# A hybrid S5, attention and mixture-of-experts block: a 22nd weight block, gather from x2, scatter summed in PSUM, shorter head, router and end

## The chip, the cores and the metric

One program on 1 core of a Trainium2 chip. The metric is the device time of one execution in microseconds (us). The kernel before was run three times: median 677.47 us, 676.79 to 678.37. About 0.2% (1.4 us) is what a measurement of this kernel can tell from no change. The engines are TensorE (PE, its weight loads PEld), VectorE (DVE, `V` in the code), ScalarE (ACT, `A`), GpSimd (POOL, `G`) and SyncE (SP, `DS`), which issues nearly all DMAs.

## The reference, cut to what matters

One block on 256 tokens of width 1024, all in fp32:

```python
h = rms_norm(x, ln1_g);  proj = h @ w_in                 # 1024 x 4096
# u -> S5 state-space mixer -> gelu -> glu;  q, k, v -> causal attention with a bias by distance, 8 heads
merged = sigmoid(gate_ssm) * (y_ssm @ w_up_ssm) + sigmoid(gate_attn) * (y_attn @ w_up_attn)
x = x + merged @ w_out
x = x + hier_moe(rms_norm(x, ln2_g), ...)
return rms_norm(x, ln_f_g)

def hier_moe(xf, ...):       # 4 groups x 8 experts, the best group, its 2 best experts
    for e in range(32):
        y = y + combine[:, e:e+1] * ((silu(xf @ w1[e]) * (xf @ w3[e])) @ w2[e])
```

The weights of the 32 experts (w1, w3: 1024 x 512, w2: 512 x 1024) are 192 MB, all of which are read whatever the router chooses.

## The kernel before

The kernel is one straight program; the order of each engine's instructions is that of the code. On-chip memory is cut into 23 blocks of 128 x 2048 fp32 (`blk`, tags r0 to r22), 1 MB each. A block has one user after another; a new user waits until the last reader of the old one is through. Most blocks serve the front stage first and the expert weights afterwards.

Front stage. `load_unit` (L734) loads one raw weight unit (1 MB of w_in, w_glu, w_up or w_out) into blocks 2 and 3 in turn, always two units ahead; its DMA on SP waits until the unit two before has been used. The first nine units of w_in are multiplied as fp32. The later sixteen units are split by ACT, DVE and POOL into a high and a low fp32r part (`split`, L699 and L702; `wtiles`, L748, takes blocks 4 and 6 or 5 and 7 in turn) and multiplied in three passes. Between the matmuls of a unit, `bg()` lets threads run for the S5 mixer, for the attention and for POOL. A table `KN` says which engine copies what and after how many steps a thread goes on.

Head. TensorE runs 24 warm-up matmuls on ones (L828). Then x times the gain goes to h32, half by ACT, half by DVE (L1523, L1525; ahead of it DVE runs the 13 instructions of `vexp`), and the first unit's sixteen matmuls follow, in four pairs of k (L1528).

Expert weights. `pump` (L765) takes the next 1 MB piece of the list: for each of eight quads (four experts each) sixteen w13 pieces (`k`, `t` for w1 or w3) and eight w2 pieces. It goes into the next of the 21 blocks in `KN['slots']`, in a ring. In the front stage `KN['pump']` says ahead of which half unit a piece is issued. As SP issues in order, a piece whose block isn't free holds back the raw loads behind it. In the expert stage every used piece pumps one more.

Router (from L1693). After the last quarter of the out matmuls, x2 is updated by DVE (L1700), squared by ACT for the norm (L1701), transposed by TensorE (`x2_tp`, L1708) and copied by ACT into x2T in block 5 (L1709); the logits follow (L1717). `rsqrt` (L704) is ten DVE instructions: a first guess from the bits and three Newton steps. Then the normalised h2 is written by ACT to block 7 (L1741), and the choice of group and experts is a chain of small DVE instructions (L1744 to L1775). Three matmuls (L1778 to L1780) count positions; `pos` is their product with the mask (L1782).

Expert stage (`moe_quads`, L1863). `pick` (L1829) compares positions with 1 to 32 and gives a 0/1 matrix; `gather` (L1837) multiplies h2 by it to give xg, the tokens of four experts, transposed; L1839 multiplies by the gain. `up13` (L1856) has four matmuls for each piece, into two banks pa and pb. Silu and product on ACT and DVE, four transposes, then w2 (L1903), and the scatter (L1918): the result goes back through DwT to tokens, and DVE adds it to x2 (L1919), four times a quad. Two PSUM tags of four banks are there: "a" (pa, pb, and others in the front stage) and "b" (all that passes through). In the last quad `final_part` squares x2 and multiplies it by the final gain on POOL (L1936), `final_end` (L1940 to L1949) has rsqrt, four products with it and four stores on SP. Loops for experts with over 32 tokens stand behind (L1957); in these runs they are not entered.

The functions of the change and what calls them:

Of the kernel before, what the change touches and what calls it, by code (L numbers as in the profile page):

```python
# [653 lines left out]
def hybrid_block(ctx, tc, x_ch, x_tok, small, consts, bc, w_in, w_glu, w_up, w_out, rel, onehot, w_rt, w13, w2,  # L654
# [79 lines left out]
    def load_unit(key, src, shape, parts=1):  # L734
        t = carve(blk(2 + n_raw[0] % 2, "raw"), shape[1:])[0]
# [5 lines left out]
        return t  # L741
# [4 lines left out]
    n_w = [0]  # L746
# [34 lines left out]
    sm = per.tile([128, SM_W], F32, name="sm")  # L781
# [12 lines left out]
    A.dma_start(sm, small)  # L794
# [443 lines left out]
    def norm1():  # L1238
# [5 lines left out]
        rsqrt(rtk, v1, t1, g1)  # L1244
# [274 lines left out]
    vexp(dt_, lst, pick_engine("vexp", "G", "GV"))  # L1519
    for pr in range(4):  # L1520
# [59 lines left out]
    for i, (kind, u) in enumerate(units):  # L1580
# [5 lines left out]
        if kind == "glu":  # L1586
# [9 lines left out]
            G.tensor_copy(trib, tri_f)  # L1596
# [134 lines left out]
    logits(0, range(4))  # L1731
# [314 lines left out]
```

## Time and profile before

| | |
|---|---|
| median of 3 runs | 677.47 us |
| profiled execution, its own time | 677.7 us |
| its span | 675.9 us, 9611 instructions |
| PE busy | 524.9 us (78%) |
| DVE, ACT, POOL busy | 219.9, 124.8, 135.1 us |
| DMA | 235.02 MB, mean 348 GB/s |
| weight pieces wslot | 191 of 1024 KB and 2 of 512 KB, median 19.8 us to landing |
| mean granted clock of TensorE | 0.869 |

The span is what the profiler saw of the program, the time what the device took. Busy shares are means over stages with different limits: the stage up to about 200 us is dense work on all engines, the rest is the stream of expert weights.

### The profile page before, as it was taken

How to read it: one execution, taken by the hardware profiler on the slowest of the kernel's cores; microseconds unless marked ns; L12 is line 12 of the kernel's file. 1: busy time of each engine (PE TensorE's matmuls, PEld its weight loads, DVE VectorE, ACT ScalarE, POOL GpSimd, SP SyncE). 2: the span in 40 equal slices, each digit the busy share in tenths (PEclk: the TensorE clock that was granted, in tenths of full speed). 3: DMA queues.
4: the chain of work that ended last, by engine and by line, in shares of the span. 5: the costliest groups of instructions: out<-in, count | busy, mean ns of one | idle time of the engine just before them, and what ended most of it. 6: DMA issues, size and time to landing. Idle time of an engine off the chain costs nothing. (4 is left out here: it accounts for less than half of the span.)

```text
span 675.9 us, 9611 instructions
## 1 busy us (share of the span) xinstructions
PE 524.9 (78%) x3931; PEld 292.3 (43%) x3931; DVE 219.9 (33%) x432; ACT 124.8 (18%) x281; POOL 135.1 (20%) x232
## 2 busy tenths in 40 slices
PE   9989999969998889696686757768766766676680
PEld 8878899859986443150041014104201400230130
DVE  5755889867785312120021011001101100120012
ACT  3362644464315010000000000001000000100021
POOL 4889455744561000000000000000000000000020
PEclk9989999998999899987689689766977976897685
DMA  7527343665899999999999999999999999999971
GB/s 264 199 87 248 125 157 126 250 250 193 324 369 423 406 422 420 421 420 422 420 421 421 421 422 421 420 422 420 422 421 421 420 420 422 420 422 421 420 317 68
DMA packets 35154, 235.02 MB, mean 348 GB/s; under 512 B 4051, under 2 KB 5244, under 8 KB 7452
## 3 DMA queue, kind: packets, MB, share of 16 engines
q1 hardware_dynamic: 34700, 232.51, 84.6%
q0 software_dynamic: 256, 1.74, 0.7%
q8 instruction: 33, 0.54, 0.3%
q14 instruction: 21, 0.17, 0.1%
q10 hardware_dynamic: 144, 0.06, 0.0%
HBM read 233.23 MB, written 2.63 MB: 349 GB/s over the span
## 5 line engine op out<-in xcount | busy, mean ns | idle before, releaser
L1856 PE MATMUL pb<-wslot,xg 128*32 128x512 f32 x512 | 87.1, 761 | 41.8 <-DMA wslot<-in_w 41.7
L1856 PE MATMUL pa<-wslot,xg 128*32 128x512 f32 x512 | 89.2, 777 | 38.2 <-DMA wslot<-in_w 38.2
L1936 POOL TENSOR_TENSOR ob<-x,xg 128x256 f32<-128x256 f32 (+1 forms) x6 | 5.3, 913 | 438.6 <-DMA wslot<-in_w 434.2
L1903 PE MATMUL py<-wslot,mt 128*32 128x256 f32 x1024 | 71.7, 421 | 24.5 <-DMA wslot<-in_w 18.9
L1889 DVE SCALAR_TENSOR_TENSOR mt<-mt,pa 128x512 f32<-128x512 f32 x8 | 5.5, 688 | 224.9 <-ACT mt L1888 224.9
L1856 PEld LDWEIGHTS pb<-wslot,xg 128*32 128x32 f32 x512 | 12.9, 120 | 114.8 <-DMA wslot<-in_w 104.9
L1903 PEld LDWEIGHTS py<-wslot,mt 128*32 128x32 f32 x1024 | 31.4, 119 | 64.6 <-DMA wslot<-in_w 31.6
L1856 PEld LDWEIGHTS pa<-wslot,xg 128*32 128x32 f32 x512 | 12.1, 120 | 100.4 <-DMA wslot<-in_w 88.1
L702 POOL TENSOR_TENSOR wl<-raw,wh 128x512 fp32r<-128x512 f32 (+1 forms) x22 | 40.3, 1836 | 33.8 <-ACT wh L699 18.5
L1919 DVE TENSOR_TENSOR x<-x,scp 128x512 f32<-128x512 f32 (+1 forms) x34 | 22.3, 657 | 58.7 <-PE scp L1918 58.7
L1839 DVE TENSOR_TENSOR xg<-xgp,sm 128x512 f32<-128x512 f32 (+1 forms) x18 | 11.4, 632 | 90.1 <-PE xgp L1837 90.1
L1918 PE MATMUL scp<-mt 128*128 128x512 f32 (+1 forms) x68 | 32.9, 609 | 7.1 <-ACT mt L1915 7.1
L1888 ACT ACTIVATE mt<-pa 128x512 f32<-128x512 f32 x8 | 4.8, 597 | 176.5 <-PE pa L1856 176.5
L1837 PEld LDWEIGHTS xgp<-mt,h 128*128 128x128 f32 x256 | 33.6, 214 | 6.3 <-issue 5.5
L1837 PE MATMUL xgp<-mt,h 128*128 128x128 f32 x256 | 35.5, 302 | 0.9 <-DVE mt L1829 0.9
L1915 ACT COPY mt<-py 128x512 f32<-128x512 f32 (+1 forms) x17 | 9.5, 561 | 125.8 <-PE py L1903 125.8
L702 DVE TENSOR_TENSOR wl<-raw,wh 128x512 fp32r<-128x512 f32 (+1 forms) x26 | 29.5, 1145 | 6.7 <-ACT wh L699 5.9
L1276 PE MATMUL inp<-hn,raw 128*128 128x256 f32 x128 | 29.8, 390 | 0.0
L1280 PE MATMUL inp<-hH,wh 128*128 128x256 f32 x112 | 28.2, 288 | 0.0
L1280 PE MATMUL inp<-hL,wh 128*128 128x256 f32 x112 | 27.6, 283 | 0.0
L1276 PEld LDWEIGHTS inp<-hn,raw 128*128 128x128 f32 x128 | 24.8, 197 | 4.0 <-DVE vu L1295 0.6
L699 ACT CAST wh<-raw 128x512 fp32r<-128x512 f32 (+1 forms) x28 | 20.7, 769 | 18.2 <-DMA raw<-in_w_out 7.9
(318 smaller groups left out, 745.6 us busy)
## 6 DMA issues: line engine op xcount, KB each, us to landing
wslot<-in_w SPq DMA_DIRECT2D x191, 1024.0 KB, 19.8
raw<-in_w_in SPq DMA_DIRECT2D x14, 1024.0 KB, 4.9
raw<-in_w_up SPq DMA_DIRECT2D x4, 1024.0 KB, 5.0
raw<-in_w_out SPq DMA_DIRECT2D x4, 1024.0 KB, 4.8
rbz<-rbd POOLq DMA_DIRECT2D x1, 1536.0 KB, 8.7
xc<-in_x_ch SPq DMA_DIRECT2D x4, 256.0 KB, 4.8
raw<-in_w_in SPq DMA_DIRECT2D x4, 256.0 KB, 5.8
raw<-in_w_in SPq DMA_DIRECT2D x2, 512.0 KB, 7.2
```

What stands on the lines that cost most here:

```text
L699: (A.copy if e is A else e.tensor_copy)(out_, in_)
L702: pick_engine(name, default, opts).tensor_tensor(out=out, in0=in0, in1=in1, op=op)
L1276: T.matmul(ps[:, 0:S], raws["in", u][:, k, c], (h32 if u < 3 else hn)[:, k], start=(k == 0), stop=(k == KD - 1))
L1280: T.matmul(ps[:, 0:S], (wh if x else wl)[:, k, c], (hH if y else hL)[:, k], start=first, stop=last)
L1837: T.matmul(ps[:, i * 128:i * 128 + 128], h2[:, b, k * 128:k * 128 + 128], Dt[:, b].rearrange("p e s -> p (e s)"), start=(b == 0), stop=(b ...
L1839: V.tensor_tensor(out=xg[:, ks[0]:ks[0] + n], in0=ps[:, 0:n * 128].rearrange("p (k n) -> p k n", k=n), in1=smc("g2", ks[0], ks[0] + n).uns ...
L1856: T.matmul(pab[t][32 * e:32 * e + 32], xg[:, k, 32 * e:32 * e + 32], w[:, e], start=(k == 0), stop=(k == KD - 1))
L1889: V.scalar_tensor_tensor(out=hid, in0=hid, scalar=1.0, in1=pab[0], op0=OP.add, op1=OP.mult)
L1903: T.matmul(py[32 * e:32 * e + 32, n % 2 * 256:n % 2 * 256 + 256], hidT[:, f, 32 * e:32 * e + 32], w[:, i, e], start=(f == 0), stop=(f == 3))
L1915: A.copy(ye[:, o % 512:o % 512 + m], py[:, o % 512:o % 512 + m])
L1918: T.matmul(ps[:, 0:m], DwT[:, b], ye[:, o % 512:o % 512 + m], start=True, stop=True)
L1919: V.tensor_tensor(out=x2[:, b, o:o + m], in0=x2[:, b, o:o + m], in1=ps[:, 0:m], op=OP.add)
```

## The change

- `rsqrt` is four instructions, the first a power of -0.5 on POOL (exponent in a new tile `mhalf`); the old one stays as `rsqrt_newton` for the first norm. An early small ACT instruction writes half of `mhalf`.
- 10 warm-ups instead of 24; `vexp` is emitted behind the first pair of k.
- `KN['pump']` is empty. `KN['after']` issues pieces right behind raw loads: 1 behind in9, 2 behind in11, 2 behind glu, 1 behind in15, 2 each behind up1 and up3, 1 behind out0, 2 behind out1, 1 behind out2; the rest up to the number of blocks follow the last out matmuls. The split blocks start with 5 and 7 instead of 4 and 6 (`nw`), and the ring has 22 blocks in a new order, block 7 among them.
- h2 is x2 itself; the norm's factor goes into the pick matrix (`Dts`). The counting matrix carries 512 on its diagonal, so that positions of chosen tokens lie above 512: the first pick reads them from PSUM, without the product with the mask. The index isn't cast to fp32.
- The first quad gathers k by k, and its first expert matmuls start after two of them.
- The scatter of quads 0 to 6 is summed in four PSUM banks; `sum_start`, in the last quad, adds them to x2 in a block of its own. The final gain is loaded in the last quad.
- The four stores go out in turn on SP and ACT, each behind its product.

```diff
+KN['pump'] = {}
+KN['nw'] = 1
+KN['warm'] = 10
+KN['SL'] = 1
+KN['after'] = {'in9': 1, 'in11': 2, 'glu': 2, 'in15': 1, 'up1': 2, 'up3': 2, 'out0': 1, 'out1': 2, 'out2': 1}
+KN['slots'] = [20, 16, 18, 17, 21, 19, 10, 11, 8, 22, 13, 15, 12, 14, 9, 3, 7, 2, 4, 0, 1, 6]
...
     def rsqrt(y, v, tmp, g):
+        G.tensor_tensor(out=y, in0=v, in1=mhalf, op=OP.pow)
+        V.scalar_tensor_tensor(out=g, in0=v, scalar=-0.5, in1=y, op0=OP.mult, op1=OP.mult)
+        V.tensor_tensor(out=tmp, in0=g, in1=y, op=OP.mult)
+        V.scalar_tensor_tensor(out=y, in0=tmp, scalar=1.5, in1=y, op0=OP.add, op1=OP.mult)
...
     def load_unit(key, src, shape, parts=1):
+        load_raw(key, src, shape, parts)
+        pump(KN["after"].get(key if isinstance(key, str) else "%s%d" % key, 0))
...
-    n_w = [0]
+    n_w = [KN["nw"]]
...
+    mhalf = sm[:, SM_W:SM_W + 2]
+    G.memset(mhalf, -0.5)
     warm = bank("warm", "a")
-    for i in range(24):
-        T.matmul(warm[:, 0:128], ones, ones, start=(i == 0), stop=(i == 23))
+    for i in range(KN["warm"]):
+        T.matmul(warm[:, 0:128], ones, ones, start=(i == 0), stop=(i == KN["warm"] - 1))
+    A.activation(out=mhalf[:, 1:2], in_=ones[:, 0:1], func=AF.Copy, scale=-0.5)
...
-    vexp(dt_, lst, pick_engine("vexp", "G", "GV"))
     for pr in range(4):
...
+        if pr == 0:
+            vexp(dt_, lst, pick_engine("vexp", "G", "GV"))
...
-            G.tensor_copy(trib, tri_f)
+            V.scalar_tensor_tensor(out=trib, in0=ident, scalar=511.0, in1=tri_f, op0=OP.mult, op1=OP.add)
+            G.tensor_scalar(out=iota512, in0=iota1, scalar1=511.0, scalar2=None, op0=OP.add)
...
-    logits(0, range(4))
+    logits(0, range(8))
     x2_tp(3, A.copy)
...
     rsqrt(rs2, v2, rw1, rw2)
-    logits(0, range(4, 8))
     logits(1, range(8))
...
-    V.tensor_copy(ixf, i8[:, :, 0:2])
...
-                    in1=ixf.unsqueeze(3).to_broadcast([128, 2, 2, 32]), op=OP.is_equal)
+                    in1=i8[:, :, 0:2].unsqueeze(3).to_broadcast([128, 2, 2, 32]), op=OP.is_equal)
...
-    V.tensor_tensor(out=pos.rearrange("p b e -> p (b e)"), in0=pp[:, 0:64], in1=msk.rearrange("p b e -> p (b e)"),
-                    op=OP.mult)
...
+    if SL:
+        xacc = [bank("xacc") for i in range(4)]
+        default_tag[0] = "a"
...
+        V.tensor_tensor(out=Dt, in0=iota512.unsqueeze(1).unsqueeze(1).to_broadcast([128, 2, 4, 32]),
+                        in1=(pos if at is None else at)[:, :, es].unsqueeze(3).to_broadcast([128, 2, 4, 32]),
+                        op=OP.is_equal)
+        if SL:
+            V.tensor_tensor(out=Dts, in0=Dt, in1=rs2.unsqueeze(2).unsqueeze(3).to_broadcast([128, 2, 4, 32]), op=OP.mult)
...
-                pick(qd)
-                gather(qd, (0, 1))
+                pick(qd, None if extra else pp[:, 0:64].rearrange("p (b e) -> p b e", b=2))
+                gather(qd, (0,))
+                gather(qd, (1,))
+                if not extra:
+                    V.tensor_copy(pos.rearrange("p b e -> p (b e)"), pp[:, 0:64])
+                up13(qd, pab, (0,))
                 gather(qd, (2, 3))
-                up13(qd, pab, (0,))
+                up13(qd, pab, (1,))
                 gather(qd, (4, 5))
-                up13(qd, pab, (1,))
                 gather(qd, (6, 7))
...
+                if last and SL:
+                    lnf_load()
+                    sum_start()
+                up13(qd, pab, range(2, 6))
+                if last and SL:
+                    lnf_rows()
+                up13(qd, pab, range(6, KD))
...
+                    if SL and not extra and not last:
+                        T.matmul(xacc[2 * b + o // 512], DwT[:, b], ye, start=(qd == qds[0]), stop=(qd == qds[-2]))
+                        continue
...
+    def sum_start():
+        fin["x"] = carve(blk(FIN[2], "xs"), (2, DM))[0]
+        for i in range(4):
+            b, n = divmod(i, 2)
+            c = slice(n * 512, n * 512 + 512)
+            V.tensor_tensor(out=fin["x"][:, b, c], in0=x2[:, b, c], in1=xacc[i], op=OP.add)
+        default_tag[0] = "b"
...
-        for b, o in ((0, 0), (0, 512), (1, 512), (1, 0)):
-            DS.dma_start(out[b * 128:(b + 1) * 128, o:o + 512], ob[:, b, o:o + 512])
+            (A if i % 2 else DS).dma_start(dst, x)
```

## Rows read from the trace of the kernel before

**Rows 1.** The page, part 2: DMA share in tenths, 40 slices.
```profile
DMA  7527343665899999999999999999999999999971
```

**Rows 2.** Waits of the SP queue: total us, times, longest.
```profile
SPq L774 <- DMA wslot<-in_w: 333.0, 158, 3.1
```

**Rows 3.** Stretches: busy us by engine, granted clock, DMA share, GB/s.
```profile
120.00:140.00 20.00, 17.52 (x233) 15.32 (x222) 15.38 (x21) 11.34 (x37) 15.36 (x16) 1.00 0.56 211
140.00:160.00 20.00, 16.15 (x102) 14.04 (x102) 14.26 (x27) 11.18 (x26) 5.95 (x11) 0.83 0.62 232
160.00:180.00 20.00, 20.00 (x169) 20.00 (x168) 15.36 (x22) 7.61 (x16) 10.63 (x9) 1.00 0.86 352
180.00:200.00 20.00, 19.69 (x120) 17.26 (x120) 17.63 (x24) 4.23 (x9) 13.40 (x12) 1.00 0.83 318
200.00:220.00 20.00, 16.61 (x97) 14.13 (x96) 12.07 (x40) 8.45 (x17) 3.83 (x4) 0.96 1.00 415
...
260.00:280.00 20.00, 17.30 (x138) 5.04 (x138) 3.42 (x6) 1.35 (x4) 0.00 (x0) 1.00 1.01 420
```

**Rows 4.** The tile wslot: from a piece's issue to its landing.
```profile
DMA to landing us min/median/max: 5.4/19.8/21.1
```

**Rows 5.** Timeline of SP's issues: start us, us, queue, line, xcount.
```profile
119.10 0.43 SPq L774 DMA_DIRECT2D wslot<-in_w  x1
...
191.34 0.80 SPq L774 DMA_DIRECT2D wslot<-in_w  x2
...
198.56 0.33 SPq L739 DMA_DIRECT2D raw<-in_w_out  x1
...
199.88 13.38 SPq L774 DMA_DIRECT2D wslot<-in_w  x8
...
226.39 13.82 SPq L774 DMA_DIRECT2D wslot<-in_w  x11
```

**Rows 6.** Timeline of the router, ahead of the first expert matmul.
```profile
211.61 0.59 ACT L1709 COPY x2T<-x2tp 128x512 f32<-128x512 f32 x1 [2.83 <-PE acc L1679]
...
213.63 2.99 PE L1717 MATMUL lgp<-mt,x2T 128*128 128x36 f32 x24
...
217.36 0.42 DVE L1744 SCALAR_TENSOR_TENSOR mt<-lgp,mt,sm 128x36 f32<-128x36 f32 x2
...
221.07 0.42 DVE L1829 TENSOR_TENSOR mt<-co,mt 128x256 f32<-128x256 f32 x1
...
221.65 3.69 PE L1837 MATMUL xgp<-mt,h 128*128 128x128 f32 x16 [0.87 <-DVE mt L1829]
...
225.27 1.06 PE L1856 MATMUL pa<-wslot,xg 128*32 128x512 f32 x8
```

**Rows 7.** Timeline of the head, and DVE at the attention's bias.
```profile
1.06 8.30 PE L828 MATMUL warm<-fs 128*128 128x128 f32 x48 [1.06 <-DVE fs L825]
...
4.46 1.28 ACT L1523 ACT_TABLE_LOAD   x1 [4.46 <-DMA xc<-in_x_ch]
...
7.31 0.61 DVE L1525 TENSOR_SCALAR h<-xc,sm 128x256 f32<-128x256 f32 x2
...
9.19 7.07 PE L1528 MATMUL inp<-h,raw 128*128 128x256 f32 x32
...
66.23 1.29 DVE L1347 SCALAR_TENSOR_TENSOR attA<-sc,attA 128x512 f32<-128x512 f32 x2 [1.25 <-DMA attA<-rbz]
```

**Rows 8.** Timeline of the end: last norm, products, stores.
```profile
661.42 0.33 DVE L1940 SCALAR_TENSOR_TENSOR mt<-mt 128x2 f32<-128x2 f32 x1 [0.74 <-ACT mt L1931]
...
663.90 1.28 DVE L1947 TENSOR_SCALAR ob<-ob,mt 128x512 f32<-128x512 f32 x3 [0.30 <-DVE mt L710]
...
664.41 3.59 SPq L1949 DMA_DIRECT2D out_dram<-ob  x4
```

**Rows 9.** POOL by form: busy us, mean ns of one, idle before.
```profile
L702 POOL TENSOR_TENSOR wl<-raw,wh 128x1024 fp32r<-128x1024 f32 x7 | 18.0, 2575 | 14.3 <-PE inp L1276 5.8 <-ACT wh L699 5.7 <-DVE wh L699 2.7
...
L899 POOL TENSOR_TENSOR fs<-fs 128x16 f32<-128x16 f32 x5 | 1.2, 239 | 0.4
```

More of the change, by code (lines that the diff above doesn't have):

```diff
@@ L648 @@
 }
+KN['pump'] = {}
[3 more added lines that the diff above has]
+KN['SL'] = 1
+KN['after'] = {'in9': 1, 'in11': 2, 'glu': 2, 'in15': 1, 'up1': 2, 'up3': 2, 'out0': 1, 'out1': 2, 'out2': 1}
+KN['slots'] = [20, 16, 18, 17, 21, 19, 10, 11, 8, 22, 13, 15, 12, 14, 9, 3, 7, 2, 4, 0, 1, 6]
 OPTS = {}
@@ L778, in pump @@
             ready[p] = t
-    sm = per.tile([128, SM_W], F32, name="sm")
+    sm = per.tile([128, SM_W + 34], F32, name="sm")
     co = per.tile([128, CO_W], F32, name="co")
@@ L793, in hybrid_block @@
     native = set(("in", u) for u in KN["nat"]) | set(KN["nat2"])
-    A.dma_start(sm, small)
+    A.dma_start(sm[:, 0:SM_W], small)
     for k in range(0, KD, 2):
@@ L1243, in norm1 @@
         V.tensor_scalar(out=v1, in0=ss1, scalar1=1.0 / DM, scalar2=EPS, op0=OP.mult, op1=OP.add)
-        rsqrt(rtk, v1, t1, g1)
+        rsqrt_newton(rtk, v1, t1, g1)
         for b in range(2):
@@ L1735, in hybrid_block @@
     rsqrt(rs2, v2, rw1, rw2)
-    logits(0, range(4, 8))
     logits(1, range(8))
     dump("x2", x2)
-    h2 = carve(blk(7, "h2"), (2, DM))[0]
-    for b in range(2):
-        A.activation(out=h2[:, b], in_=x2[:, b], func=AF.Copy, scale=rs2[:, b:b + 1])
+    SL, fin = KN["SL"], {"x": x2}
+    Dts = hid[:, 0:256].rearrange("p (b e s) -> p b e s", b=2, e=4) if SL else Dt
+    if SL:
+        h2 = x2
+    else:
+        h2 = carve(blk(7, "h2"), (2, DM))[0]
+        for b in range(2):
+            A.activation(out=h2[:, b], in_=x2[:, b], func=AF.Copy, scale=rs2[:, b:b + 1])
     lg = pt("lg", [128, 2, 36])
@@ L1815, in rounds, with lnf_load @@
         V.tensor_copy(nri, nrf)
-    xg, lnf = carve(blk(5, "xg"), (KD, 128), (DM,))
-    G.dma_start(lnf[0:1], ln_f)
+    if SL:
+        xacc = [bank("xacc") for i in range(4)]
+        default_tag[0] = "a"
+        xg, = carve(blk(5, "xg"), (KD, 128))
+    else:
+        xg, lnf = carve(blk(5, "xg"), (KD, 128), (DM,))
+        G.dma_start(lnf[0:1], ln_f)
+        fin["lnf"] = lnf
+    def lnf_load():
+        fin["lnf"] = carve(blk(FIN[1], "lnf"), (DM,))[0]
+        G.dma_start(fin["lnf"][0:1], ln_f)
     def lnf_rows():
+        lnf = fin["lnf"]
         for n in range(2):
@@ L1881, in moe_quads @@
                     rounds()
-                    lnf_rows()
+                    if not SL:
+                        lnf_rows()
                 up13(qd, pab, (4, 5, 6, 7))
@@ L1886, in moe_quads @@
                 back(qd)
-                up13(qd, pab, range(2, KD))
+                if last and SL:
[3 more added lines that the diff above has]
+                if last and SL:
+                    lnf_rows()
+                up13(qd, pab, range(6, KD))
             A.activation(out=hid, in_=pab[0], func=AF.Tanh, scale=0.5)
@@ L1935, in final_part @@
         for b in range(2):
-            G.tensor_tensor(out=ob[:, b, o:o + m], in0=x2[:, b, o:o + m], in1=lnf[:, o:o + m], op=OP.mult)
+            G.tensor_tensor(out=ob[:, b, o:o + m], in0=x[:, b, o:o + m], in1=lnf[:, o:o + m], op=OP.mult)
     def final_end():
@@ L1941, in final_end @@
         rsqrt(rs3, v3, rw1, rw2)
-        for b, o in ((0, 0), (1, 512), (0, 512), (1, 0)):
-            x = ob[:, b, o:o + 512]
-            if (b, o) == (1, 512):
+        for i, (b, o) in enumerate(((0, 0), (1, 512), (0, 512), (1, 0))):
+            x, dst = ob[:, b, o:o + 512], out[b * 128:(b + 1) * 128, o:o + 512]
+            if i == 1:
                 A.activation(out=x, in_=x, func=AF.Copy, scale=rs3[:, b:b + 1])
@@ L1947, in final_end @@
                 V.tensor_scalar(out=x, in0=x, scalar1=rs3[:, b:b + 1], scalar2=None, op0=OP.mult)
-        for b, o in ((0, 0), (0, 512), (1, 512), (1, 0)):
-            DS.dma_start(out[b * 128:(b + 1) * 128, o:o + 512], ob[:, b, o:o + 512])
-    FIN = [SLOTS[(n_pieces - NSLOT) % NSLOT]]
+            (A if i % 2 else DS).dma_start(dst, x)
+    FIN = [SLOTS[(n_pieces - NSLOT + i) % NSLOT] for i in range(3 if SL else 1)]
     moe_quads(range(NQ_RUN))
```

26 lines of the change are left out of this document (13 added, 13 removed).

## The prediction, made before the changed kernel was run

> **What bounds the kernel now.** I read the page's DMA line first: from the 12th of 40 slices on the DMA engines stand at 9 until the last two slices [rows 1]. Then the SP queue's own waits: 333.0 us, 158 times, are L774 waiting for an earlier weight piece [rows 2]. Then stretches: in 260 to 280 the DMA share is 1.01 at 420 GB/s [rows 3], so a 1 MB piece (1.049 MB) takes 2.50 us, and the 192 pieces of the experts take 480 of the 675.9 us. A piece lands 5.4 us after its issue at best and 19.8 in the median [rows 4]: 5.4 is 2.5 of transfer behind 2.9 of start and completion, and 19.8 is eight pieces in flight. In the expert stage only bytes count; an engine that gets faster there gives nothing. Two things can move the end: DMA time left idle before that stage, and what follows the last landing.
>
> Idle before: the DMA shares 0.56, 0.62, 0.86 and 0.83 between 120 and 200 us [rows 3] leave 20 x (0.44 + 0.38 + 0.14 + 0.17) = 22.6 us unused. By 191.7 SP has issued 11 pieces, the last raw load goes out at 198.56, and ten more pieces by 213.26. Then SP stands still until 226.39: all 21 blocks are full [rows 5]. It goes on when the first w13 piece has been used, 225.27 + 1.06 = 226.33 [rows 6]; call this moment R. Piece 22 therefore lands at 226.39 + 5.4 = 231.8. The eleven transfers issued from 198.56 on last about 198.6 + 2.4 + 11 x 2.5 = 228.5, so the rings are all but dry when R comes; share 1.00 in 200 to 220 [rows 3] says they were full until then. From R on, the time is R + 5.4 + (pieces left - 1) x 2.5 + tail, as long as a changed kernel also runs dry at R.
>
> **The change, part by part.**
>
> Head. The warm-ups are 24 matmuls in 8.30 us, and the first real matmul starts where they end, at 9.19 [rows 7]. That is 0.35 each in the mean, the early ones more; ten at 0.43 end at 5.4. What is late then: ScalarE's first scaling waits for a table load of 1.28 us until 5.76; the new small activation draws that load ahead of the data. DVE's first scaling starts at 7.31 behind the 13 instructions of vexp; it now goes ahead of vexp [rows 7]. Then vexp (13 short steps, about 2.7 us) holds the second DVE scaling until about 8.0. So the first pair of k runs from 5.4 to 7.8, the second starts at about 8.0, and three pairs of 1.77 us (7.07 / 4) end at 13.3 instead of 9.19 + 7.07 = 16.26. That is 2.9 us. If the clock is granted later than here, the first pair runs at half rate and 1.6 is left. TensorE has hardly a gap from there to 216, and most raw loads are released by it or by the splits that feed it, so the shift should travel; but the bias load of the attention hangs on POOL, which does not shift: DVE already waits 1.25 us for it at 66.23 [rows 7]. I take 2.4 of 2.9; bounds 0 and 2.9.
>
> Pieces behind raw loads. 14 pieces instead of 11 are issued before the last raw load, into the 22.6 idle us. The three extra (7.5 us) only count as far as blocks allow: with 22 blocks SP stops after piece 22, and the rings then run dry about 224.4 on the old clock (198.6 + 2.4 + 9 x 2.5 = 223.5 for the raw load and 8 pieces, and about 0.9 of gaps, because the last blocks come free only while the out matmuls end). R plus 2.9 is later, so the block count binds and the gain is one piece, 2.5 us, plus whatever R gains. Raw loads behind two pieces may land up to 2.5 us later; the places are early (in13) and late (out2), and their splits start a microsecond or more after landing, so I cost it at nothing; the price without that cover is a rival.
>
> Router. Before, the ScalarE copies of x2T wait 2.83 us for the last out matmul [rows 6], because block 5 is still a split weight; with the split blocks swapped they don't. But the transposes of the last quarter now come behind sixteen logit passes: 213.63 + 2.99 ended at 216.62 [rows 6], and I get about 216.8 after. Behind the long rsqrt lg ran from 217.36 to 217.78; with the short one its factor is ready at about 215.5, so lg ends when the logits do, at 217.2: 0.6 gained. The index cast (0.2) and the product for pos (0.26) leave the path, the product with rs2 (0.42, as the comparison at 221.07) enters it: net 0. Then the gather: 16 passes in 3.69 us, 0.23 each at half clock, all before the first expert matmul at 225.27 [rows 6]. Now only two k, eight passes, stand ahead of it: 1.8 saved. If the clock is still at half when the first four expert matmuls run, they take about 1.9 instead of 1.06: 0.9 lost. R moves by 0.6 + 1.8 - 0.9 = 1.5; bounds 1 and 3.3 (full clock in the gather).
>
> Scatter in PSUM, pick, lnf, sum_start. Four DVE additions of 0.7 us a quad go, one product of 0.42 comes, and only two banks circulate beside pa and pb; all lies under a DMA stream that keeps eight pieces ahead: 0. lnf is loaded 20 pieces, 50 us, before the end: 0.
>
> Tail. From v3 (661.42 + 0.33) to the factors (663.90 less the 0.30 of idle) ten DVE instructions take 1.85 us [rows 8]. The new chain has three of 0.2 and one on POOL. The trace has no power on POOL; a small two-input operation there takes 0.24 us, its longest 2.58 [rows 9]. A 128x2 operand is nearest to the small one; with two handovers I take 0.4, so 1.0 us instead of 1.85: 0.8 saved (bounds 0.8 and -1.5). The four stores leave SP one behind the other, 664.41 to 668.00 [rows 8], though DVE's last product ends at 663.90 + 1.28 = 665.18; an issue that waits for nothing is 0.33 to 0.43 [rows 5], four of them 1.5, so one stood about 2.1 us. With two queues the last issue ends 0.4 behind the last product, 665.6 in today's times, if nothing stands: 2.4 saved; if SP's second store stands again, about 0.7. I take 1.2. The Trainium skill (DMA: Bandwidth & Descriptors, "Issuing engines are not separate DMA queues") says that issuing from several engines saves only the sequencers' issue time, usually small beside the transfer; by it this term would be near 0 and the sum 670.2, but the 3.59 us of rows 8 are issue time, and not small.
>
> Sum, against the profiled execution (677.7, span 675.9, 1.8 around it): 2.4 + 2.5 + 1.5 + 0.8 + 1.2 = 8.4, so 669.3. The median of the three runs lies 0.2 lower: 669.0 (677.47 - 8.4 = 669.07).
>
> **Rivals.**
> *The head's shift is absorbed* by POOL's chain and the bias load: against it, TensorE itself is nearly gapless; for it, DVE's wait at 66.23. 669.0 + 2.4 = 671.4.
> *More than that*: full clock in the gather (R by 3.3 instead of 1.5) and no standing store (+1.2): 666.0. For it, the shorter idle of TensorE before the gather.
> *Late raw loads*: two places on TensorE's path pay a piece each, 5.0: 674.0. Against it, splits don't start at landing; for it, two of the raw loads come out while two pieces stand ahead of them in the rings.
> *Slower: the power on POOL.* It stands on the path twice. In the router it is free up to 1.8 us (by my estimate startable at 214.5, its result wanted at 216.9 after three short DVE steps), at the end from 0.4 on. At POOL's longest row, 2.58, the time is 669.0 + 0.8 + 2.2 = 672.0; from P - 1.8 + P - 0.4 = 8.4, so P = 5.3, the kernel is slower than before; at 6.3 it takes 679.4. No POOL row is near that. The Trainium skill (GPSIMD Engine Reference, "Instruction dispatch") puts the first call of a freshly loaded kernel at about 6 us; by that, paid once in the router, an estimate from that page is 673.2, and no run here shows such a load.
> *It doesn't do what it says*: the 22nd block fills no sooner, because a piece waits for a block and holds a raw load behind it in SP's order. Gains of head and tail are eaten: about 676.5.
>
> **Chances.** Forecast 0.53 (its own range 667 to 671), head absorbed 0.15, more 0.13, late raw loads 0.09, slow power 0.06 (slower in 0.04 of it), not as said 0.04 (half of it no change or slower). Range 665.0 to 674.0: it leaves out some of "more" and the last two. About 0.2% is what a measurement here can tell, 1.4 us. Faster 0.92, same 0.03, slower 0.05.
>
> **What would show it.** The first L1528 matmul near 5.4 and the first L1276 near 13.3; SP with 14 pieces ahead of the last raw load and 8 behind it; the first L1856 matmul about 3.9 earlier (2.4 + 1.5) than 225.27, and a dip of DMA share below 1 just after it; the last landing about 6.4 earlier than now; from the last landing to the end 2 us less. The forecast is wrong if the first expert matmul comes no earlier than 224, if POOL's power takes over 2 us, or if gaps for raw weights appear on TensorE between 90 and 212.

## The result, and the profile after

The changed kernel takes 667.5 us (median of four, 664.9 to 670.0) against 677.8 before: ratio 0.9856, 95% interval 0.9835 to 0.9876. The forecast was 669.0 with a range of 665 to 674. So the time came out, 1.5 us from the likeliest value. The working behind it did not: two of its five terms (head and stores) do not show in the medians, a third has a cost that was not counted, and about half of the gain comes from a line of the diff that the prediction passed over. What follows takes that apart.

The profiled execution is the slowest of the four: 669.96 us, span 668.2 against 675.9, so 7.7 us, where the medians gained 10.3. The split below is of these two executions and leaves 2.6 us of the medians' gain open; what other profiles say is set beside it. It goes by SP's issues. From the 37th piece on (counting from 1) SP issues at the pace of the landings, one for one, up to the last:

| stretch | before | after | gain | forecast |
|---|---|---|---|---|
| start of the span to the issue of piece 37 | 250.03 | 247.31 | 2.7 | 6.4 (head 2.4, 22nd block 2.5, router 1.5) |
| piece 37 to the last issue (156 later) | 390.5 | 385.4 | 5.2 | 0 |
| last issue to the end of the span | 35.4 | 35.5 | -0.2 | 2.0 (root 0.8, stores 1.2) |

The middle line is the surprise. Here is the page's rate (GB/s in 40 slices), first of the kernel before, then of the one after:

```profile
GB/s 264 199 87 248 125 157 126 250 250 193 324 369 423 406 422 420 421 420 422 420 421 421 421 422 421 420 422 420 422 421 421 420 420 422 420 422 421 420 317 68
```

```profile
GB/s 307 183 64 252 127 222 127 350 218 231 324 370 325 352 427 425 427 425 428 426 428 424 430 424 429 424 430 424 428 425 428 425 429 425 428 425 426 427 312 70
```

From the 15th slice on 420 to 422 have become 424 to 430, with the DMA engines full in both. The trace's packet records say how: between 280 and 640 us an 8 KB packet takes 309 ns after, nearly without exception (18,709 packets); before, 73% of them take longer, mostly 311 to 322, and the mean is 313.4 (here and below without some twenty packets a profile of over 400 ns). 1.4% of the 385 us are 5.4 us.

The head. Columns of a timeline: start, length, engine, line, operation, out<-in, count, [idle before, and who ended it]:

```profile
1.05 4.26 PE L848 MATMUL warm<-fs 128*128 128x128 f32 x20 [1.05 <-DVE fs L843]
5.15 1.89 PE L1548 MATMUL inp<-h,raw 128*128 128x256 f32 x8
7.89 5.45 PE L1548 MATMUL inp<-h,raw 128*128 128x256 f32 x24 [0.85 <-DVE h L1545]
13.18 4.05 PE L1297 MATMUL inp<-h,raw 128*128 128x256 f32 x18
...
43.32 0.90 PE L1074 MATMUL m1p<-co,W1e 128*128 128x128 f32 x3 [2.99 <-ACT W1e L708]
44.01 6.16 PE L1297 MATMUL inp<-hn,raw 128*128 128x256 f32 x16
50.01 0.60 PE L1074 MATMUL m1p<-co,W1e 128*128 128x128 f32 x4
```

The first real matmul comes at 5.15 (9.19 before [rows 7], 5.4 forecast) and the second unit at 13.18 (13.3 forecast), 2.9 us earlier than before. The second unit and the place at 40 to 50 us before:

```profile
16.10 8.15 PE L1276 MATMUL inp<-h,raw 128*128 128x256 f32 x37
...
44.68 0.90 PE L1053 MATMUL m1p<-co,W1e 128*128 128x128 f32 x3 [2.39 <-ACT W1e L699]
45.38 4.75 PE L1276 MATMUL inp<-hn,raw 128*128 128x256 f32 x16
49.96 0.60 PE L1053 MATMUL m1p<-co,W1e 128*128 128x128 f32 x4
```

Behind a wait for the factors of the state-space mixer (SSM; tile W1e) 1.36 us of the 2.9 are left (44.68 to 43.32), and at 50.0 nothing: the sixteen matmuls took 6.16 us instead of 4.75. The stretches say why: mean granted clock 0.57 after and 0.72 before in 44 to 50 us, so more of it at the lower of the two levels (1.2 instead of 2.4 GHz, called half clock here), in both behind a wait of TensorE (2.99 and 2.39 us). From there to 90 us SP's raw loads go out within 0.1 us of those before (50.21 and 50.15, 89.14 and 89.08). The stretches before, then after (columns as in [rows 3]):

```profile
44.00:50.00 6.00, 5.32 (x20) 4.54 (x21) 4.66 (x10) 1.89 (x7) 5.09 (x8) 0.72 0.02 5
```

```profile
44.00:50.00 6.00, 6.00 (x18) 4.79 (x17) 4.88 (x9) 0.59 (x2) 4.44 (x7) 0.57 0.01 2
```

The raw loads. The page's issue lines give the median from issue to landing of the four raw loads of w_out: 4.8 us before, 7.5 after:

```profile
raw<-in_w_out SPq DMA_DIRECT2D x4, 1024.0 KB, 7.5
```

One of them in the timeline after, issued at 189.64 behind two pieces (185.60, 187.04):

```profile
189.64 0.33 SPq L758 DMA_DIRECT2D raw<-in_w_out  x1
...
199.46 0.43 DVE L708 CAST wh<-raw 128x512 fp32r<-128x512 f32 x1 [2.24 <-DMA raw<-in_w_out]
199.51 0.84 POOL L708 CAST wh<-raw 128x512 fp32r<-128x512 f32 x1 [3.31 <-DMA raw<-in_w_out]
...
200.40 0.50 PE L1703 MATMUL acc<-wh,mH 128*128 128x512 f32 x1 [1.31 <-POOL wh L708]
```

The splits wait until 199.46, 9.8 us after the issue, and TensorE waits for the split. This is the gap that the prediction named as proof against itself. From the issue of the first raw load of w_out to the end of the out matmuls there were 33.3 us before (178.70 to 211.95), and 35.5 after (177.85 to 213.38): 2.3 lost. First the two rows before, then the two after:

```profile
178.70 5.72 SPq L739 DMA_DIRECT2D raw<-in_w_out  x2
211.33 0.62 PE L1679 MATMUL acc<-wl,mH 128*128 128x512 f32 x2
```

```profile
177.85 0.33 SPq L758 DMA_DIRECT2D raw<-in_w_out  x1
212.76 0.62 PE L1703 MATMUL acc<-wl,mH 128*128 128x512 f32 x2
```

The router after, which answers to [rows 6]:

```profile
213.66 1.87 PE L1741 MATMUL lgp<-mt,x2T 128*128 128x36 f32 x16
...
215.54 0.72 POOL L714 TENSOR_TENSOR mt<-mt,sm 128x2 f32<-128x2 f32 x1 [7.23 <-DVE mt L1758]
...
217.79 0.26 DVE L1772 SCALAR_TENSOR_TENSOR mt<-lgp,mt,sm 128x36 f32<-128x36 f32 x1 [0.58 <-PE lgp L1741]
...
220.88 0.42 DVE L1864 TENSOR_TENSOR mt<-sm,pp 128x256 f32<-128x256 f32 x1 [0.33 <-PE pp L1806]
221.33 0.42 DVE L1868 TENSOR_TENSOR mt<-mt 128x256 f32<-128x256 f32 x1
221.90 2.04 PE L1875 MATMUL xgp<-mt,x 128*128 128x128 f32 x8 [1.06 <-DVE mt L1868]
...
223.88 1.94 PE L1894 MATMUL pa<-wslot,xg 128*32 128x512 f32 x8
```

From the end of the out matmuls to the first expert matmul there are 10.5 us instead of 13.3, 2.8 gained; the first eight instructions there then run at half clock, 1.94 instead of 1.06. SP goes on at 225.87 instead of 226.39 [rows 5]; this is the moment R of the prediction, when the first used piece frees a block.

The stretches say what became of the idle DMA time. In 120 to 200 us the share rose from 0.72 (mean of four stretches of [rows 3]) to 0.80, 6.4 us more of transfer. In 200 to 220 it fell from 1.00 [rows 3] to 0.88 and in 220 to 260 from 1.01 to 0.97, 2.4 and 1.6 us given back. Before, then after:

```profile
220.00:260.00 40.00, 36.11 (x339) 18.96 (x338) 10.39 (x32) 3.94 (x9) 0.00 (x0) 0.94 1.01 415
```

```profile
120.00:200.00 80.00, 72.98 (x627) 66.38 (x626) 60.84 (x93) 34.18 (x86) 41.57 (x43) 0.96 0.80 305
200.00:220.00 20.00, 17.21 (x96) 14.06 (x97) 10.94 (x32) 6.60 (x15) 6.16 (x6) 1.00 0.88 339
220.00:260.00 40.00, 35.46 (x337) 18.09 (x337) 10.42 (x34) 3.04 (x7) 0.00 (x0) 0.92 0.97 396
```

In finer stretches after, the rings run dry in two places: at 204 to 206 us, where SP has stood 5.6 us at a piece whose block waits for one of POOL's splits, and just behind R, as forecast:

```profile
204.00:206.00 2.00, 2.00 (x10) 1.61 (x10) 0.47 (x1) 1.12 (x3) 1.04 (x1) 1.00 0.13 53
226.00:228.00 2.00, 2.00 (x16) 0.92 (x8) 0.00 (x0) 0.00 (x0) 0.00 (x0) 0.84 0.60 98
```

The end, which answers to [rows 8]:

```profile
654.75 0.33 DVE L1998 SCALAR_TENSOR_TENSOR mt<-mt 128x2 f32<-128x2 f32 x1 [0.75 <-ACT mt L1989]
655.16 0.72 POOL L714 TENSOR_TENSOR mt<-mt,sm 128x2 f32<-128x2 f32 x1
...
656.50 1.28 DVE L2005 TENSOR_SCALAR ob<-ob,mt 128x512 f32<-128x512 f32 x3
657.02 0.82 SPq L2006 DMA_DIRECT2D out_dram<-ob  x2
657.30 0.85 ACTq L2006 DMA_DIRECT2D out_dram<-ob  x2
```

The last quad's first scatter, before and after:

```profile
650.03 1.98 PE L1918 MATMUL scp<-mt 128*128 128x512 f32 x4 [0.77 <-ACT mt L1915]
```

```profile
642.80 3.78 PE L1969 MATMUL scp<-mt 128*128 128x512 f32 x4 [0.76 <-ACT mt L1963]
```

From the last operation on v3 (the mean square of the last norm; 654.75 after) to VectorE's first product there are 1.75 us instead of 2.48, and no store stands in its queue. Yet from that operation to the end of the span there are 13.4 us, and 14.5 before.

### The profile page after: what moved, and what is told of

Its sections match the earlier page's. It is cut to its first block, busy times and chain, and to the rows that moved or that the text cites. A ratio compares the mean times of both kernels' runs of the same rounds, so it can differ in the third digit from the quotient of the medians.

```text
span 668.2 us, 9545 instructions
## 1 busy us (share of the span) xinstructions
PE 525.3 (79%) x3903; PEld 288.8 (43%) x3903; DVE 204.5 (31%) x403; ACT 122.9 (18%) x280; POOL 134.4 (20%) x235
## 5 line engine op out<-in xcount | busy, mean ns | idle before, releaser
L1894 PE MATMUL pb<-wslot,xg 128*32 128x512 f32 x512 | 88.8, 774 | 36.3 <-DMA wslot<-in_w 35.7
L1894 PEld LDWEIGHTS pb<-wslot,xg 128*32 128x32 f32 x512 | 13.2, 120 | 109.7 <-DMA wslot<-in_w 95.1
L1877 DVE TENSOR_TENSOR xg<-xgp,sm 128x512 f32<-128x512 f32 (+2 forms) x19 | 11.5, 608 | 84.6 <-PE xgp L1875 84.6
L1875 PEld LDWEIGHTS xgp<-mt,x 128*128 128x128 f32 x256 | 33.3, 213 | 7.0 <-issue 6.1
L1875 PE MATMUL xgp<-mt,x 128*128 128x128 f32 x256 | 35.3, 301 | 1.1 <-DVE mt L1868 1.1
L1297 PE MATMUL inp<-hn,raw 128*128 128x256 f32 x128 | 31.3, 404 | 0.8 <-DVE vu L1316 0.8
L1966 PE MATMUL xacc<-mt 128*128 128x512 f32 x56 | 27.1, 606 | 5.3 <-ACT mt L1963 5.3
L711 DVE TENSOR_TENSOR wl<-raw,wh 128x512 fp32r<-128x512 f32 (+1 forms) x26 | 28.1, 1091 | 10.2 <-ACT wh L708 8.0
L708 ACT CAST wh<-raw 128x512 fp32r<-128x512 f32 (+1 forms) x28 | 20.6, 768 | 20.7 <-DMA raw<-in_w_out 10.4
L1301 PEld LDWEIGHTS inp<-hH,wh 128*128 128x128 f32 x112 | 21.4, 191 | 0.3 <-issue 0.2
```

Of the source, the lines that this page charges most:

```text
L708: (A.copy if e is A else e.tensor_copy)(out_, in_)
L711: pick_engine(name, default, opts).tensor_tensor(out=out, in0=in0, in1=in1, op=op)
L1297: T.matmul(ps[:, 0:S], raws["in", u][:, k, c], (h32 if u < 3 else hn)[:, k], start=(k == 0), stop=(k == KD - 1))
L1301: T.matmul(ps[:, 0:S], (wh if x else wl)[:, k, c], (hH if y else hL)[:, k], start=first, stop=last)
L1875: T.matmul(ps[:, i * 128:i * 128 + 128], h2[:, b, k * 128:k * 128 + 128], Dts[:, b].rearrange("p e s -> p (e s)"), start=(b == 0), stop=(b ...
L1877: V.tensor_tensor(out=xg[:, ks[0]:ks[0] + n], in0=ps[:, 0:n * 128].rearrange("p (k n) -> p k n", k=n), in1=smc("g2", ks[0], ks[0] + n).uns ...
```

## The experiments

For the 5.2 us of the middle line two theories stood against each other at first: that the scatter in PSUM (four VectorE additions a quad less) makes the stream faster, and that it depends on how the packets fall in one execution. Neither held. For the 2.7 instead of 6.4 us: late raw loads, or a stream that hides them.

**one_store_queue** (the changed kernel)

```diff
-            (A if i % 2 else DS).dma_start(dst, x)
+            DS.dma_start(dst, x)
```

> The changed kernel (667.5 us) with all four stores issued by SP again. In the profile after, from the operation that closes v3 to the end of the span are 13.45 us, before 14.5; of the 1.05 us the short root chain has about 0.4. Theory (the second queue is worth the rest, 0.65): 668.2 us, 14.1 us from v3 to the end. The forecast's size (1.2): 668.7 us. Rival (several issuers save nothing, the landings set the end): 667.5 us, and 13.45 us from v3 to the end. Beside it: if the faster stream (8 KB packets of 309 ns, 426 GB/s) belongs to the changed kernel and not to one execution of it, this profile shows 426 GB/s from 260 us on as well.

Measured: 667.33 us, ratio 0.9856 (0.9836 to 0.9877), the same as the changed kernel; two such medians cannot tell 1 us apart. From v3 to the end of the span 12.9 us, against 13.2 to 13.7 in the nine profiles of the changed kernel and its variants with two queues. The last issue ends 3.4 us behind the start of the first product instead of 1.65, but the last store's packet then comes 2.6 us behind that issue instead of 4.4. So by the profiles the rival holds here: what the second queue saves at the issue is spent in the transfer. The stream runs at 426 GB/s here as well, so it is no matter of one execution.

**before_two_queues** (the kernel before, stores by SP and ScalarE in turn)

```diff
-        for b, o in ((0, 0), (0, 512), (1, 512), (1, 0)):
-            DS.dma_start(out[...], ob[:, b, o:o + 512])
+        for i, (b, o) in enumerate(((0, 0), (1, 512), (0, 512), (1, 0))):
+            (A if i % 2 else DS).dma_start(out[...], ob[:, b, o:o + 512])
```

> The kernel before with one edit: the four stores go out by SP and ScalarE in turn. Theory: a gain of 0.7 us, 677.1 us. The forecast's size: 676.6 us. Rival (the landings set the end): 677.8 us. Beside it, for the stream: if 420 GB/s (packets of 309 to 322 ns, mean 314) belongs to the kernel before, it is there again from 240 us on; if it belongs to one execution, this one can show 309 ns and 426 GB/s, and would then be about 5 us shorter.

Measured: 676.03 us, ratio 0.9988 (0.9973 to 1.0003): a gain of 0.6 us, not told from no change, nor from the forecast's 1.2 (the interval reaches 1.8). Its profile has 12.8 us from v3 to the end of the span, the three of the kernel before with one queue 13.7 to 14.5; so in that kernel the second queue may be worth something. The stream is at 421 GB/s, packets of 313.4 ns in the mean. So the rate goes with the kernel.

**dve_scatter_21** (the changed kernel)

```diff
-KN['SL'] = 1
+KN['SL'] = 0
-KN['slots'] = [..., 14, 9, 3, 7, 2, 4, 0, 1, 6]
+KN['slots'] = [..., 14, 9, 3, 2, 4, 0, 1, 6]
```

> The changed kernel with 21 blocks, the scaled copy of x2 in the 22nd, and the scatter added by VectorE quad by quad, as before; head, raw-load places, root and stores stay changed. Theory 1 (the stream's 426 GB/s instead of 420 comes of the scatter in PSUM, that is of four VectorE additions a quad less): 420 GB/s from 260 us on, 667.5 + 2.5 (one piece) + 0.5 (two copies) + 5.1 = 675.6 us. Theory 2 (the rate depends on how the packets of the 16 engines fall together in an execution, not on the scatter): 426 GB/s or a value between, 670.5 us. Rival for the block: the 22nd block fills no sooner, so taking it away costs nothing: 667.5 to 668 us.

Measured: 669.89 us, ratio 0.9891 (0.9870 to 0.9912), and 427 GB/s. The scatter in PSUM is not what speeds the stream. Against 667.33 in the same runs the 22nd block, with the copies of x2 that it drops, is worth 2.6 us; forecast 2.5. The two intervals overlap, but SP's issues agree: from R to the issue of piece 37 there are 24.4 us here, and 20.6 to 22.3 in the nine profiles of the changed kernel and its variants with 22 blocks.

**twelve_ahead** (the changed kernel)

```diff
-KN['after'] = {..., 'up3': 2, 'out0': 1, 'out1': 2, 'out2': 1}
+KN['after'] = {..., 'up3': 2, 'out0': 1, 'out1': 1}
```

> The changed kernel with 12 pieces ahead of the last raw load instead of 14: one behind out1 instead of two, none behind out2. Theory (two late raw loads ate the head's shift): the raw load of out2 lands about 5.5 us after its issue instead of 9.8, the gap of 1.3 us on TensorE at 200 us goes, the first expert matmul comes at about 222.3 instead of 223.9, and the time is 667.5 - 1.2 = 666.3 us. Rival (bytes: the two pieces now stand behind the last raw load and keep the rings full past the first used piece): no gain, 667.5 to 668.5 us.

Measured: 667.09 us, ratio 0.9863 (0.9845 to 0.9882): no gain that can be told. In its profile the mechanism shows plainly: 33.2 us from the first raw load of w_out to the end of the out matmuls, as before the change, first expert matmul at 220.08, and no dip of the DMA share:

```profile
200.00:220.00 20.00, 16.09 (x98) 14.08 (x96) 10.68 (x33) 6.60 (x15) 3.24 (x3) 0.88 1.01 426
220.00:260.00 40.00, 37.12 (x345) 17.50 (x348) 8.77 (x29) 3.04 (x7) 0.00 (x0) 0.93 1.01 426
```

Its profiled execution, 665.19 us, is the fastest of its four; that of the changed kernel was the slowest. Late raw loads are shown, what they cost in the median is not.

What was left of the diff for the stream was small. `mhalf` is not a tile of its own: it and a table of the numbers above 512 are 34 more columns of the tile `sm`, which lies ahead of all blocks.

```diff
-    sm = per.tile([128, SM_W], F32, name="sm")
+    sm = per.tile([128, SM_W + 34], F32, name="sm")
```

In the program's layout that moves every block from 128 to 256 modulo 512 bytes within its partition. (The few tiles between `sm` and the blocks move too; the stream writes none of them.) Three kernels test the address alone.

**before_plus_128_bytes** (the kernel before)

```diff
-    sm = per.tile([128, SM_W], F32, name="sm")
+    sm = per.tile([128, SM_W + 32], F32, name="sm")
-    A.dma_start(sm, small)
+    A.dma_start(sm[:, 0:SM_W], small)
```

> The kernel before with one edit: the tile sm, which lies ahead of all blocks in SBUF, is 32 floats wider, so that every 8 KB block starts 128 bytes per partition further on (at 256 modulo 512 instead of 128, as in the changed kernel, where sm grew by 34 floats). Nothing uses the new columns. Theory (the address of the blocks sets the packet time): 8 KB packets of 309 ns from 240 us on, 426 GB/s, and 676.6 - 5.2 = 671.4 us. Rival (the order of the blocks or the places of the pieces between the raw loads set it): packets of 309 to 322 ns again, 420 GB/s, 676.6 us.

Measured: 672.71 us, ratio 0.9926 (0.9901 to 0.9951), 4.9 us faster. All but 0.2% of the packets take 309 ns. Its stretch, beside 420 GB/s in [rows 3]:

```profile
260.00:280.00 20.00, 17.29 (x145) 5.14 (x138) 3.42 (x6) 1.55 (x3) 0.00 (x0) 1.00 1.01 426
```

**before_plus_64_bytes** (the same with `SM_W + 16`)

> The kernel before with sm 16 floats wider: the blocks start 64 bytes further on, at 192 modulo 512 (64 modulo 128). If what counts is that a block starts at a multiple of 256 bytes, it stays slow or gets slower: 420 GB/s or less, 676.6 us or more. If the old address, 128 modulo 512, was the only bad one: 426 GB/s, 671.4 us. If the address doesn't count: 420 GB/s, 676.6 us.

Measured: 677.23 us, ratio 1.0003 (0.9984 to 1.0022); 93% of the packets slow, mean 313.7 ns:

```profile
260.00:280.00 20.00, 17.46 (x138) 5.04 (x136) 3.42 (x6) 0.97 (x2) 0.00 (x0) 0.97 1.01 421
```

**after_plus_128_bytes** (the changed kernel with `SM_W + 66`, blocks at 384 modulo 512)

> The changed kernel with sm another 32 floats wider: the blocks start at 384 modulo 512 (128 modulo 256) instead of 256. Theory (blocks off a multiple of 256 bytes take longer packets): 420 GB/s again, 667.4 + 5.2 = 672.6 us, so that the rest of the change is worth only 4 of its 9 us. Rival (the address doesn't count, or only 128 modulo 512 is bad): 426 GB/s, 667.4 us.

Measured: 673.29 us, ratio 0.9942 (0.9922 to 0.9963): 5.9 us slower than the changed kernel. 75% of the packets slow, mean 313.5 ns:

```profile
260.00:280.00 20.00, 18.11 (x154) 5.44 (x152) 2.14 (x4) 1.57 (x3) 0.00 (x0) 0.97 1.01 421
```

So the address is the cause, by putting it right in the one kernel and wrong in the other. Fast at 256 modulo 512, slow at 128, 192 and 384: of the four that ran, the one that is a multiple of 256. The Trainium skill (DMA: Bandwidth & Descriptors, "How a descriptor splits into AXI transactions") says that each transaction starts at a multiple of 256 bytes, and that a descriptor which starts between two of them pays for the unused bytes in front. An estimate from it: 8192 + 128 bytes instead of 8192 make 309 ns x 1.0156 = 313.8, and the runs show 313.4 and 313.5. At 192 modulo 512 the same sum with 192 bytes gives 316.2, and the run shows 313.7; there the page's count is not what was measured. The page speaks of bytes fetched, while here the destination moved, and its charge would fall on every row, while at 128 and 384 a quarter of the packets take 309 ns. So the address is shown to be the cause, and how it costs time is not. A start at 0 modulo 512 was not tried.

**old_head** (the changed kernel)

```diff
-KN['warm'] = 10
+KN['warm'] = 24
-    A.activation(out=mhalf[:, 1:2], in_=ones[:, 0:1], func=AF.Copy, scale=-0.5)
...
+    vexp(dt_, lst, pick_engine("vexp", "G", "GV"))
     for pr in range(4):
...
-        if pr == 0:
-            vexp(dt_, lst, pick_engine("vexp", "G", "GV"))
```

> The changed kernel with the old head: 24 warm-up matmuls, vexp ahead of the first loop, no early small activation. The first expert matmul is at 223.9 us in the profile after. Theory (the head's 2.9 us was mostly eaten by the late raw loads of out2 and out3, whose places hang on SP's queue): the first expert matmul at about 224.5, 667.4 + 0.5 = 667.9 us. The forecast's size (2.4 of 2.9 travel): 226.3 us there, 669.8 us. Rival (the rings are full when the first piece is used, so an earlier start gives nothing): 667.4 us.

Measured: 667.11 us, ratio 0.9847 (0.9821 to 0.9873): the shorter head is worth nothing that can be told, and the forecast's 669.8 lies outside the interval (up to 669.0). First expert matmul at 224.26, near the theory's 224.5; the first raw load of w_out at 177.78, against 177.85 with the new head.

**newton_roots** (the changed kernel)

```diff
-    rsqrt(rs2, v2, rw1, rw2)
+    rsqrt_newton(rs2, v2, rw1, rw2)
-        rsqrt(rs3, v3, rw1, rw2)
+        rsqrt_newton(rs3, v3, rw1, rw2)
```

> The changed kernel with all reciprocal roots made on VectorE in ten or so steps again, none on POOL. In the profile after the power on POOL took 0.72 us, and the chain with it 1.45 us instead of 1.85 at the end; in the router, the second of the two logit scalings started at 217.79, right behind the last logits. Theory: 0.4 us at the end and up to 0.5 in the router: 667.4 + 0.7 = 668.1 us. The forecast's sizes (0.8 at the end, 0.6 in the router): 668.8 us. Rival (the end's chain stands beside other waits): 667.4 us.

Measured: 668.93 us, ratio 0.9872 (0.9847 to 0.9898), which does not part the three cases. The trace says more: from v3 to the first product 2.27 us instead of 1.75, and in the router 10.5 us from the out matmuls to the first expert matmul, as with POOL's power. So the power is worth 0.5 us at the end and nothing in the router, where the last logits decide.

**thirteen_ahead** (the changed kernel)

```diff
-KN['after'] = {..., 'out0': 1, 'out1': 2, 'out2': 1}
+KN['after'] = {..., 'out0': 1, 'out1': 1, 'out2': 1}
```

> The changed kernel with 13 pieces ahead of the last raw load: one behind each of out0, out1 and out2, so that the raw load of out2 has one piece less in front of it. With 12 ahead the out matmuls ended 3.8 us earlier than in the profile after and the DMA share stayed at 1.0 past the first used piece: from then on the rings were the limit. Theory (what counts is the sooner of two: blocks filled and first piece used; 13 ahead gives both): the raw load of out2 lands within 7 us, out matmuls end by 211 us, first expert matmul by 222, no stretch of the DMA share below 0.9 between 200 and 232, 666.0 us. Rival (the rings are never the limit before the first piece is used, and what is gained there is lost in the stream): 667.4 us.

Measured: 667.51 us (664.3 to 668.9), ratio 0.9851 (0.9820 to 0.9881). The profile has what was expected (out matmuls end at 210.07, first expert matmul at 220.57), the median has not: again the profiled execution, 664.33, is the fastest of five. The theory's 666.0 is not shown.

**thirteen_held_clock** (as the last, and)

```diff
     logits(1, range(8))
+    dum = bank("dum", "a")
+    for i in range(12):
+        T.matmul(dum[:, 0:128], ident, ident, start=True, stop=True)
...
+    for i in range(4):
+        T.matmul(dum[:, 0:128], ident, ident, start=True, stop=True)
     pos = pt("pos", [128, 2, 32])
```

> As the kernel with 13 pieces ahead, and twelve small matmuls of no use behind the last logits, four more behind the counting of positions, so that TensorE is not idle in the 2.85 and 1.06 us in which it waits for the router. In every profile so far the granted clock was at half for 6.8 us from the wait on, and the first two gathers (2.04 us for eight passes) and the first four expert matmuls (1.94 us for eight) fell into it. Theory: full clock there, the first piece used 1.7 us earlier than with 13 ahead alone, 664.8 us. Rival (the rings are full by then, so an earlier first use frees a block that nothing waits for): no gain over 13 ahead, 666.0 us. If the small matmuls run into the positions' matmuls: 0.2 us lost.

Measured: 664.83 us (663.7 to 666.9), ratio 0.9815 (0.9786 to 0.9844), 2.7 us below the last. The waits are filled, and the gather and the first expert matmuls run at the upper level (a matmul in fp32 is two records, so twelve are x24):

```profile
216.03 2.92 PE L1763 MATMUL dum<-co 128*128 128x128 f32 x24
...
219.12 1.14 PE L1810 MATMUL dum<-co 128*128 128x128 f32 x8
220.34 1.13 PE L1879 MATMUL xgp<-mt,x 128*128 128x128 f32 x8
221.48 1.06 PE L1898 MATMUL pa<-wslot,xg 128*32 128x512 f32 x8
```

2.04 and 1.94 us have become 1.13 and 1.06, the 1.7 us of the theory. The two kernels' intervals overlap, so how much of the 2.7 is the clock's is not settled by the medians.

**held_twice** (as the last, and small matmuls in the wait at 40 us)

```diff
             for i in range(4):
                 q4, ri = divmod(h * 4 + i, 2)
+                if (j, h, i) == (0, 0, 1):
+                    d1 = bank("d1", "a")
+                    for _ in range(11):
+                        T.matmul(d1[:, 0:128], ident, ident, start=True, stop=True)
```

> As the kernel with 13 pieces ahead and the held clock in the router, and eleven more small matmuls in the wait of 2.99 us that TensorE has at 40.3 to 43.3 us for the SSM's factors. In the profile after the granted clock was at half from 42.3 to 49.2 (before: 44.2 to 47.7), and of the 2.9 us by which the head was earlier 1.36 were left behind that wait and none at 50.2. Theory (the wait eats half of the head's shift and the half clock behind it the rest): full clock there, the third quarter of raw loads and all that follows 1.7 us earlier, 663.1 us. Rival (other chains, above all POOL's and the bias load at 60 us, hold the stage anyway): 664.8 us.

Measured: 662.22 us (661.1 to 663.7), ratio 0.9762 (0.9733 to 0.9792): the fastest of all, 16 us under the kernel before, its interval clear of the changed kernel's. Its six runs (661.1 to 663.7) lie under the five of the kernel without these matmuls (663.7 to 666.9). The wait's length is as it was, its effect on the clock is gone:

```profile
40.21 2.62 PE L1077 MATMUL d<-co 128*128 128x128 f32 x22
43.38 0.55 PE L1078 MATMUL m1p<-co,W1e 128*128 128x128 f32 x3 [0.56 <-ACT W1e L708]
43.77 3.62 PE L1301 MATMUL inp<-hn,raw 128*128 128x256 f32 x16
```

```profile
44.00:50.00 6.00, 6.00 (x31) 5.31 (x30) 5.23 (x9) 1.51 (x4) 4.54 (x7) 1.00 0.30 85
```

The sixteen matmuls take 3.62 us; they took 6.16 in the profile after and 5.02 in thirteen_held_clock, from which this kernel differs. The next raw load goes out at 47.41, against 48.85 there: 1.4 us. At the first raw load of w_out it is 1.9 us ahead (176.78 against 178.64), but seven other profiles with the same front stage lie between 176.4 and 179.1 at that place. So 1.4 us behind the wait are shown, and the theory's 1.7 us fit the medians (664.8 to 662.2); how much of it arrives in one execution is not.

## Why the time was right and the working was not

**Head, 2.4 forecast; 0.8 in the two profiles, nothing that can be told in the medians.** The failing words are "so the shift should travel". The first 13 us are right to 0.3 us, and the bounds had 0. The rival "the head's shift is absorbed" is what happened, only 20 us earlier than it placed it: not at the bias load at 66 us but at the wait for the SSM's factors at 43, which keeps its own time, and at the half clock behind it. "TensorE has hardly a gap" was a misreading: the wait of 2.39 us stood in the trace of the kernel before. How long the clock stays low there differs between profiles of kernels with the same front stage (3.4 and 0 us in those of the kernel before, 6.8 and 3.4 with the new head). The next raw load goes out at 48.5 in the two profiles of the kernel before without half clock there and at 49.7 and 50.2 in the two with 3.4 us; so this is a part of the scatter of 4 to 5 us between executions, not shown to be all of it. In the seven profiles with the new head, this wait left empty and 3.4 us at half clock it goes out at 48.8 to 49.4, against 50.3 with the old head: about 1 us is left there.

**Pieces behind raw loads, 2.5 forecast.** The counts are right: 14 ahead, 8 behind, the block count binds, 2.6 us by the comparison and 2.2 in the two profiles (R to piece 37: 23.6 before, 21.4 after). The failing step is "so I cost it at nothing" for the raw loads: they landed up to 5 us late, and 2.3 us of it reached TensorE; a split of POOL also held back a piece, and the rings ran dry at 204 to 206 us, which they do not in twelve_ahead. That is the rival "late raw loads", given 0.09; it took place beside the forecast's mechanism, not instead of it.

**Router, 1.5 forecast, 1.9 found** (2.8 in the chain less 0.9 at half clock). The two k ahead of the first expert matmul gave 1.6 of the 2.8 (1.8 forecast), and the half clock there came as priced. The other 1.2 lie ahead of the gather, where 0.6 was forecast for the root. They are not the root's: newton_roots has the same 10.5 us. Which edit gave them was not tested.

R itself: 0.8 (head) - 2.3 (raw loads) + 2.8 - 0.9 = 0.4, measured 0.5 (226.39 to 225.87), forecast 3.9. The first expert matmul at 223.88 is a hair ahead of the 224 that was named as the limit.

**Scatter in PSUM, 0 forecast, 0 found**, in the sense that dve_scatter_21 has the same stream.

**Root at the end, 0.8 forecast, 0.73 found** (2.48 to 1.75, of which newton_roots leaves 0.5 to the power). POOL's power took 0.72 us, not 0.4, and the "slow power" rival is out.

**Stores, 1.2 forecast, nothing found in the changed kernel.** The issue time was saved as counted, 4.1 to 1.65 us behind the first product. The step that fails is that the end follows the last issue: it follows the last packet, which came 6.4 us behind the first product before and 6.0 after. (In the other profiles: 5.4, 5.6 and 6.0 with one queue, 4.8 to 6.1 with two. For the kernel before, 1.2 us is neither shown nor out.) Here the rule of the Trainium skill (DMA: Bandwidth & Descriptors, "Issuing engines are not separate DMA queues"), weighed and set aside in the prediction, was the better one. In the profiled execution the last quad took a further 1.2 us (last piece's packet to v3: 5.2 us instead of 4.0): four scatter matmuls at half clock took 3.78 us instead of 1.98, and when that packet came TensorE had 32 matmuls left instead of 8. So the end as a whole gained nothing there. That is this execution's own: from the last issue to the end of the span the nine other profiles of the changed kernel and its variants have 33.8 to 34.4 us, the three of the kernel before with one queue 34.8 to 35.4. About 0.9 of the 2.0 is the usual gain, near what the root gives.

**Not in the sum at all: 5 us for the address of the blocks.** The forecast's 8.4 was 6.4 + 2.0; found in the two profiles were 2.7 - 0.2, and 5.2 from elsewhere. That the sum stood is luck: a gain that nobody had seen is about as large as the gains that were lost. With the blocks at a slow start as before, the change is worth 0.58% or 4.3 us, half of the forecast's 8.4 (after_plus_128_bytes, 673.3 us, at the upper edge of the range).

## What to carry to other kernels

Where a stream of weights sets the time, look at where its buffers start: 8 KB rows that started at 256 modulo 512 bytes moved at 426 GB/s, those at 128, 192 and 384 at 421, and one widened tile ahead of them decides it. Follow a shift along the path to the first engine that does not shift, before it goes into a sum; and when a sum comes out right, check its terms. Where TensorE waits 3 us for another engine ahead of dense work, small matmuls that nothing uses can be worth as much as work that was saved: held_twice gains 5.3 us on the changed kernel (662.2 against 667.5) with 27 of them and one digit of a table, of which the digit alone (thirteen_ahead) showed no gain.

## What was not expected of the hardware

An 8 KB packet into SBUF takes 309 ns at a block start of 256 modulo 512 bytes, and 313.4 to 313.7 in the mean at 128, 192 and 384 modulo 512. It shows where the rings have been full for long, from about 240 us on; from 100 to 210 us the kernel before, too, has 309 for 89% of its packets.

Behind the wait at 40 us, where it was left empty, TensorE's clock was at half for 6.8 us in the profile after, for 3.4 in ten others, and not at all in two (before_two_queues and before_plus_64_bytes); in held_twice, where it was filled, not at all either. In all twelve profiles in which the router's wait was left empty, the clock was at half for 6.8 us or more from there on; in the two in which it was filled, never.

Two stores at once on two queues land later each: last packet 3.2 to 4.5 us behind the last issue, against 1.5 to 2.6 with one queue.
